# Odd-layer queries and keys: one 512-column matmul for both halves of the tokens, joined by a strided VectorE sum

## The chip, the core and the metric

The kernel runs on one core of a Trainium2 chip. The metric is device time in microseconds, the median of the runs shown. One more execution was taken with the hardware profiler; its own time stands in the table below.

## The reference, cut to what matters

The program is a four-stage encoder trunk over 256 tokens of 1024 features, in float32: an even layer (neighbourhood attention and latent attention), an MLP, an odd layer (three groups of dilated attention), a second MLP. The change touches the projection of the odd layer:

```python
def odd_mixer(xn, w_in, w_o, cos_f, sin_f):
    hcat = (xn @ w_in).reshape(b, s, DIL_GROUPS, 3, DIL_HEADS, HEAD_DIM)
    q = apply_rope(hcat[:, :, :, 0], cos_f, sin_f)
    k = apply_rope(hcat[:, :, :, 1], cos_f, sin_f)
    v = hcat[:, :, :, 2]
    return dilated_attention(q, k, v) @ w_o
```

`apply_rope` rotates pairs of features by the tokens' cosines and sines; `dilated_attention` computes scores, a softmax per group and the weighted values, and mixes the three groups by their softmax denominators.

## The kernel before

Every matrix product is made of three matmuls in a reduced float32 format. Each operand is split into a high half (the rounded value) and a low half (the rest), and `mm3` adds high x high, high x low and low x high into one PSUM bank:

```python
def mm3(o, sh, sl, mh, ml, first, last):
    nc.tensor.matmul(o, sh, mh, start=first, stop=False)
    nc.tensor.matmul(o, sh, ml, start=False, stop=False)
    nc.tensor.matmul(o, sl, mh, start=False, stop=last)
```

The tokens' halves are `xh` and `xl`. Weights come from memory as `raw` tiles in the fixed order of the list `specs`; each is split in four pieces, of which ScalarE writes the high half `whi` (L167) and VectorE the low half `wlo` (L168). Three pairs `whi`, `wlo` exist, so a weight's split waits until TensorE has finished with the weight three places earlier.

The odd layer works in eight units of two heads. Each unit has three query/key weights (b = 0, 1, 2: the queries and keys of the first group, the queries of the other two groups, their keys) and two value weights. A query/key weight gives two results of 128 features x 256 tokens, f = 0 and f = 1, each a chain of eight `mm3` over the eight blocks of features (k); both lie in one PSUM bank, 256 columns each. Then `rope` runs: ScalarE copies four blocks of 32 partitions from the bank into `sw` (L812, L813), VectorE multiplies the bank by the cosines into `r1` (L815) and `sw` by the sines (L816), and adds the two into `q0` (with a split, for b = 0), `q12` or `k12` (L818, L821, L825). The value weights are the moving operand of 384 columns. While TensorE makes the projections of one unit, the attention of the unit before is woven in by `weave`: scores (L180, L848), softmax on VectorE and ScalarE (L855 to L859), transposes of the probabilities (L866) with their copies (L868), and the products with the values (L881, L886) one unit later. On each engine the instructions run in the order that the scheduler gave them when the program was built. Projections and products with the values take turns in four PSUM banks named `acc`.

Of the kernel before, what the change touches and what calls it, by code (L numbers as in the profile page):

```python
# [19 lines left out]
ALU = mybir.AluOpType  # L20
# [24 lines left out]
def trunk(ctx, tc, a, out):  # L45
# [17 lines left out]
    def half_tile(pool, name, bufs, tag="half"):  # L63
        return pool.tile([P, KT, T], F32R, tag=tag, name=name, bufs=bufs)

    def quarter_pair(name):
        return [act.tile([P, KT // 2, T], F32R, tag="quarter", name=name + v, bufs=4) for v in "hl"]
# [107 lines left out]
    def two_heads(o, hi, lo, ts):  # L175

        for n, (y, z) in enumerate(((hi, hi), (hi, lo), (lo, hi))):
            for j in range(2):
                pb = slice(64 * j, 64 * j + 64)
                nc.tensor.matmul(o[j], y[pb, 0, ts], z[pb, 1, :], start=n == 0, stop=n == 2)  # L180
# [23 lines left out]
    def prepare(k, n, xT):  # L204

        hi, lo, gk = xT[0][:, k, :], xT[1][:, k, :], gains[:, n * KT + k:n * KT + k + 1]
        return (lambda: nc.scalar.activation(hi, x[:, k, :], AF.Copy, scale=gk).ins,
                lambda: nc.vector.scalar_tensor_tensor(lo, x[:, k, :], gk, hi.bitcast(F32), ALU.mult, ALU.subtract).ins)
# [62 lines left out]
    def hand_over(accs, last, n, scale=None):  # L271

        xT = half_tile(act, "xh", 2), half_tile(act, "xl", 2)
# [21 lines left out]
    def onto(accs, w, c, v, m, first, last, fbs):  # L295

        for fb in fbs:
            cs = slice(c + fb * P, c + fb * P + P)
            o = accs[fb // 2][:, (fb % 2) * T:(fb % 2) * T + T]
            mm3(o, w[0][:, cs], w[1][:, cs], m[0][v], m[1][v], first and fb % 2 == 0, last and fb % 2 == 1)  # L300

    ALL = slice(None)

    def out_steps(accs, mixed, wo, k):

        def step(fbs):
            if k // 2 not in wo:
                wo[k // 2] = weight()
            onto(accs, wo[k // 2], (k % 2) * D, (ALL, k % 4), mixed[k // 4], k == 0, k == KT - 1, fbs)
        return [lambda fbs=fbs: step(fbs) for fbs in (range(0, 4), range(4, 8))]  # L310

    def out_last(accs, mixed, wo):

        def step(b):
            for k in (6, 7):
                if 3 not in wo:
                    wo[3] = weight()
                onto(accs, wo[3], (k % 2) * D, (ALL, k % 4), mixed[k // 4], False, k == KT - 1, (2 * b, 2 * b + 1))
        return [lambda b=b: step(b) for b in range(4)]

    def mlp(mp, xT, invert, tail, make_down, beside=lambda j: None):
# [4 lines left out]
        def up(j):  # L326
# [4 lines left out]
            for ks in ranges:  # L331
                for f in range(2):
                    for k in ks:
                        c = slice(k * 256 + f * P, k * 256 + f * P + P)
                        mm3(pu[:, f * T:(f + 1) * T], w[0][:, c], w[1][:, c], xT[0][:, k, :], xT[1][:, k, :],
# [5 lines left out]
            hs[j] = tuple(mp.tile([P, 512], F32R, tag=n, name=n, bufs=4) for n in ("hh", "hl"))  # L341
            split(*hs[j], h)
# [15 lines left out]
    def mlp_between(mp, xT, s):  # L358
        def down(accs, hs):
            def step(j, w, f, fbs=range(8)):  # L360
                onto(accs, w, f * D, (ALL, slice(f * T, f * T + T)), hs[j], (j, f) == (0, 0), (j, f) == (15, 1), fbs)
# [11 lines left out]
    def finish(mp, xT, s):  # L373
# [7 lines left out]
        def mm(acc, hs, j, w, f, t, c0, c1, first, last):  # L381
            tk, c = slice(f * T + t * P, f * T + (t + 1) * P), slice(f * D + c0, f * D + c1)
            mm3(acc, hs[j][0][:, tk], hs[j][1][:, tk], w[0][:, c], w[1][:, c], first, last)
# [64 lines left out]
    def even(ep):  # L448
        xT = xh, xl = half_tile(act, "xh", 2), half_tile(act, "xl", 2)
# [28 lines left out]
        cT_h, cT_l = quarter_pair("c")  # L478
# [84 lines left out]
        def qk_steps(c):  # L563
            hold = {}

            def step(f, half):
                if not hold:
                    hold["w"], hold["p"] = weight(), bank("acc" if c else "w")
                (wh, wl), pq = hold["w"], hold["p"]
                for k in range(4 * half, 4 * half + 4):  # L570
                    ws = slice(k * 256 + f * P, k * 256 + f * P + P)
                    mm3(pq[:, f * T:(f + 1) * T], wh[:, ws], wl[:, ws], xh[:, k, :], xl[:, k, :], k == 0, k == KT - 1)
                if f == 1 and half == 1:
                    th, tl = (ep.tile([P, 2, T], F32R, tag=n, name=n, bufs=2) for n in ("qk_h", "qk_l"))
                    q32 = scratch([2, T], "q32")
                    nc.vector.tensor_tensor(q32, pq.rearrange("p (f n) -> p f n", f=2), both, op=ALU.mult)
                    split(th, tl, q32)
                    qk[c] = th, tl
# [7 lines left out]
        def heads_transposed(n, t, h, src):  # L586
# [4 lines left out]
            split(mT[n][0][0:96, hs, tok(t)], mT[n][1][0:96, hs, tok(t)], pt[0:96].rearrange("p (i n) -> p i n", i=4))  # L591

        def uq_steps():
            hold, src = {}, {}

            def gemm(t, h):
                if not hold:
                    hold["w"] = weight()
                    mT["q"] = half_tile(ep, "qh", 2, "mq"), half_tile(ep, "ql", 2, "mq")
# [16 lines left out]
        def ukv_steps():  # L616
            hold, src = {}, {}

            def gemm(t, h):
                if not hold:  # L620
                    hold["w"] = weight()
                    mT["k"] = half_tile(ep, "kh", 2, "mk"), half_tile(ep, "kl", 2, "mk")
# [27 lines left out]
        def scores(n):  # L650
# [5 lines left out]
            if kind == 0:  # L656
                two_heads(sb, *qk[hp], tok(t))
            else:
                for j in range(2):
                    h = 2 * hp + j  # L660
                    (qh, ql), (kh, kl) = mT["q"], mT["k"]
                    mm3(sb[:, j], qh[0:96, h, tok(t)], ql[0:96, h, tok(t)], kh[0:96, h, :], kl[0:96, h, :], True, True)
# [24 lines left out]
        def mix(n):  # L687
# [11 lines left out]
            split(*(z[:, hp, tok(t)] for z in mixed[kind]), pvo[:, 0:P])  # L699
# [47 lines left out]
    def odd(op, xT, s):  # L747
        xh, xl = xT
# [13 lines left out]
        def unit_tiles(u):  # L762
            d = {"k12": k12[u % 2]}
            for n, shape, dt in (("q0h", [P, 2, T], F32R), ("q0l", [P, 2, T], F32R), ("q12", [P, 2, T], F32),
# [29 lines left out]
        def qk_steps(d):  # L794
# [4 lines left out]
            def gemm(b, f, half):  # L799
                if f == 0 and half == 0:  # L800
                    hold["w"], hold["p"] = weight(), bank("acc")
                (wh, wl), pq = hold["w"], hold["p"]
                for k in range(4 * half, 4 * half + 4):
                    ws = slice((f * KT + k) * P, (f * KT + k + 1) * P)
                    mm3(pq[:, f * T:(f + 1) * T], wh[:, ws], wl[:, ws], xh[:, k, :], xl[:, k, :], k == 0, k == KT - 1)
                if f == 1 and half == 1:
                    rope(b, pq)

            def rope(b, pq):
                sw, r1 = scratch([512], "sw"), scratch([2, T], "r1")  # L810
                for r in range(0, P, 64):
                    nc.scalar.copy(sw[r:r + 32], pq[r + 32:r + 64])  # L812
                    nc.scalar.copy(sw[r + 32:r + 64], pq[r:r + 32])  # L813
                sw = sw.rearrange("p (f n) -> p f n", f=2)
                nc.vector.tensor_tensor(r1, pq.rearrange("p (f n) -> p f n", f=2), cosT.unsqueeze(1).broadcast_to([P, 2, T]), op=ALU.mult)  # L815
# [19 lines left out]
        def attention(u, d, other, pause=2):  # L835
# [4 lines left out]
            def scores():  # L840
                ss = {(i, j): bank("w") for i in range(NT) for j in range(2)}
                for i in range(NT):
                    two_heads([ss[i, j][:, 0:T] for j in range(2)], d["q0h"], d["q0l"], tok(i))
# [29 lines left out]
        def mix(u, d, out_tag):  # L873
# [14 lines left out]
            split(*(z[:, u % 4, :] for z in mixed[u // 4]), pvo[:, 0:T])  # L888
# [127 lines left out]
```

## Time and profile before

| what | us |
|---|---|
| median of 3 runs (lowest, highest) | 760.87 (760.02, 761.33) |
| the profiled execution, span from first to last instruction | 759.4 |
| TensorE busy in it | 750.6 |
| VectorE busy | 506.4 |
| ScalarE busy | 499.3 |
| odd layer, from its first to its last matmul of a projection | 302.6 to 542.6 |

The profiler gives the span alone; the median of the runs lies 1.5 us above it. Matmuls overlap in the trace: the time from one start to the next tells what a matmul takes of TensorE, and its own duration is a latency. VectorE's and ScalarE's instructions overlap a little too.

### The profile page before, as it was taken

To read this page: it belongs to the slowest core of one execution; us is meant where nothing else is said; L and a number is where in the kernel's file an instruction comes from. 1 tells how busy PE (TensorE), PEld (TensorE's weight loads), DVE (VectorE), ACT (ScalarE), POOL (GpSimd) and SP (SyncE) were. 2 spreads that over 40 slices of the span, in tenths; PEclk is the share of its full clock that TensorE was granted. 3 is DMA by queue.
4 is the path that set the end of the run, shared out by engine and by line. 5 is a ranking of instruction groups with operands and counts; after the bars stand their busy time and mean duration, and the time that the engine had idled before them with its cause. 6 is when DMAs were issued, how large, how long until landed. Compare 5 with 4: busy or idle time off the path is not lost.

```text
span 759.4 us, 14578 instructions
## 1 busy us (share of the span) xinstructions
PE 750.6 (99%) x5898; PEld 717.1 (94%) x5898; DVE 506.4 (67%) x1033; ACT 499.3 (66%) x1057; POOL 9.5 (1%) x22
## 2 busy tenths in 40 slices
PE   8999999999999999999999999999999999999996
PEld 6898899999999999999999999999999899899895
DVE  6778859646545557887787677786858555555564
ACT  6778977445435435888988889889856554554541
POOL 0100000000000001000000000000000000000000
PEclk9999999999999999999999999999999999999999
DMA  8863334454455544643444444544554555455501
GB/s 280 310 223 139 112 111 162 173 200 177 179 186 179 191 150 170 228 154 136 162 148 153 154 145 169 180 141 163 184 213 148 185 196 176 179 201 174 187 28 55
DMA packets 22818, 129.13 MB, mean 170 GB/s; under 512 B 2912, under 2 KB 5472, under 8 KB 9824
## 3 DMA queue, kind: packets, MB, share of 16 engines
q1 hardware_dynamic: 22464, 127.94, 47.8%
q8 instruction: 46, 0.75, 0.4%
q10 hardware_dynamic: 288, 0.28, 0.1%
q14 instruction: 20, 0.16, 0.1%
HBM read 127.16 MB, written 1.05 MB: 169 GB/s over the span
## 4 chain that ended last, share of the span: by engine, by line
PE 96%; ACT 1%; issue 1%; DMA 1%; DVE 1%; SPq 0%; POOLq 0%; POOL 0%
PE acc L171 21%; PE acc L172 20%; PE acc L173 20%; PE w L171 9%; PE w L172 9%; PE w L173 9%; PE w L180 1%; PE w L866 1%; PE w L683 1%; PE w L848 1%; PE acc L881 1%; PE w L697 1%; DMA raw<-in_w_c 1%; PE w L589 1%; PE acc L697 0%
## 5 line engine op out<-in xcount | busy, mean ns | idle before, releaser
L168 DVE TENSOR_TENSOR wlo<-raw,whi 128x512 fp32r<-128x512 f32 (+3 forms) x488 | 307.0, 663 | 171.9 <-ACT whi L167 171.1
L167 ACT CAST whi<-raw 128x512 fp32r<-128x512 f32 (+3 forms) x488 | 268.6, 599 | 200.0 <-issue 173.8
L172 PE MATMUL w<-xl,whi 128*128 128x256 f32 x528 | 149.2, 283 | 0.0
L173 PE MATMUL w<-xh,wlo 128*128 128x256 f32 x528 | 148.8, 282 | 0.0
L171 PE MATMUL w<-xh,whi 128*128 128x256 f32 x528 | 148.8, 282 | 0.0
L171 PE MATMUL acc<-xh,whi 128*128 128x256 f32 x432 | 125.4, 290 | 0.0
L173 PE MATMUL acc<-xh,wlo 128*128 128x256 f32 x432 | 121.8, 282 | 0.0
L172 PE MATMUL acc<-xl,whi 128*128 128x256 f32 x432 | 121.5, 281 | 0.0
L171 PEld LDWEIGHTS w<-xh,whi 128*128 128x128 f32 x528 | 99.6, 189 | 0.6
L172 PEld LDWEIGHTS w<-xl,whi 128*128 128x128 f32 x528 | 99.2, 188 | 0.6
L173 PEld LDWEIGHTS w<-xh,wlo 128*128 128x128 f32 x528 | 99.7, 189 | 0.0
L171 PEld LDWEIGHTS acc<-xh,whi 128*128 128x128 f32 x432 | 81.1, 188 | 1.3 <-issue 0.3
L172 PEld LDWEIGHTS acc<-xl,whi 128*128 128x128 f32 x432 | 81.8, 189 | 0.0
L173 PEld LDWEIGHTS acc<-xh,wlo 128*128 128x128 f32 x432 | 81.2, 188 | 0.0
L171 PE MATMUL acc<-hh,whi 128*128 128x256 f32 x256 | 72.6, 284 | 0.0
L172 PE MATMUL acc<-hl,whi 128*128 128x256 f32 x256 | 72.4, 283 | 0.0
L173 PE MATMUL acc<-hh,wlo 128*128 128x256 f32 x256 | 72.4, 283 | 0.0
L171 PE MATMUL acc<-whi,xh 128*128 128x384 f32 (+2 forms) x160 | 56.7, 354 | 1.2 <-ACT whi L167 1.2
L172 PE MATMUL acc<-wlo,xh 128*128 128x384 f32 (+2 forms) x160 | 55.9, 349 | 0.2 <-DVE wlo L168 0.2
L173 PE MATMUL acc<-whi,xl 128*128 128x384 f32 (+2 forms) x160 | 55.6, 347 | 0.0
L171 PEld LDWEIGHTS acc<-hh,whi 128*128 128x128 f32 x256 | 49.1, 192 | 0.0
L172 PEld LDWEIGHTS acc<-hl,whi 128*128 128x128 f32 x256 | 49.1, 192 | 0.0
(202 smaller groups left out, 1287.7 us busy)
## 6 DMA issues: line engine op xcount, KB each, us to landing
raw<-in_w SPq DMA_DIRECT2D x64, 1024.0 KB, 4.8
raw<-in_w_oqk SPq DMA_DIRECT2D x24, 1024.0 KB, 4.8
raw<-in_w_ov SPq DMA_DIRECT2D x16, 768.0 KB, 4.3
raw<-in_w_qk SPq DMA_DIRECT2D x4, 1024.0 KB, 10.3
raw<-in_w_oe SPq DMA_DIRECT2D x4, 1024.0 KB, 5.3
raw<-in_w_oo SPq DMA_DIRECT2D x4, 1024.0 KB, 4.8
bias<-in_rpb SPq DMA_DIRECT2D x8, 256.0 KB, 3.7
raw<-in_w_c SPq DMA_DIRECT2D x8, 208.0 KB, 4.9
```

Source lines behind the costliest of these rows:

```text
L167: a = nc.scalar.copy(hi, src).ins
L168: return a, (eng or nc.vector).tensor_tensor(lo, src, hi.bitcast(F32), op=ALU.subtract).ins
L171: nc.tensor.matmul(o, sh, mh, start=first, stop=False)
L172: nc.tensor.matmul(o, sh, ml, start=False, stop=False)
L173: nc.tensor.matmul(o, sl, mh, start=False, stop=last)
L180: nc.tensor.matmul(o[j], y[pb, 0, ts], z[pb, 1, :], start=n == 0, stop=n == 2)
L589: nc.tensor.transpose(pt[0:96, i * P:(i + 1) * P], src[:, i, :], ident)
L683: nc.tensor.transpose(pt[:, b * P:(b + 1) * P], pp[:, b // 2, (b % 2) * P:(b % 2 + 1) * P], ident)
L697: nc.tensor.matmul(pvo[64 * j:64 * j + 64, 0:P], v[:, kk, h * 64:(h + 1) * 64], pts[:, 2 * j + kk, :], start=kk == 0, stop=kk == NT - 1)
L848: nc.tensor.matmul(ss[i, j][rows, T:T + P], d["q12"][:, j, i * P + 64 * c:i * P + 64 * c + 64], d["k12"][:, j, 2 * i + c, :], start=True, ...
L866: nc.tensor.transpose(pt[:, b * P:(b + 1) * P], pp[:, b * P:(b + 1) * P], ident)
L881: nc.tensor.matmul(pvo[cs, tok(i)], d["v0"][:, kk, cs], pts[j][:, kk, :], start=kk == 0, stop=False)
```

## The change

Four things are changed.

1. High and low halves that were two tiles become one tile with a dimension of two, in all stages (`pair_tile`, `halves`). Blocks of 256 columns are then read and written at twice the step. The instructions of the other stages stay the same in kind, size and order.
2. In the odd layer's query/key products, `mm2` takes the place of `mm3`: one matmul of 512 columns takes the high weights against the tokens' high and low halves, which lie side by side, into the whole bank; a second of 256 columns adds low weights x high tokens to the bank's left half.
3. The two halves of the bank must be added: `joined`, one VectorE reduction of 256 pairs that stand 256 elements apart in PSUM, writes the sum to a scratch tile in SBUF.
4. f = 0 and f = 1 have a bank each, so two banks and two reductions per weight; `rope` then reads the scratch tile in SBUF instead of the bank.

```diff
+    def pair_tile(pool, n, name, bufs, tag):
+
+        return pool.tile([P, n, 2, T], F32R, tag=tag, name=name, bufs=bufs)
...
+    def halves(z):
+
+        return (z[:, 0, :], z[:, 1, :]) if len(z.shape) == 3 else (z[:, :, 0, :], z[:, :, 1, :])
...
+    def mm2(o, sh, sl, m, first, last):
+
+        both = lambda: nc.tensor.matmul(o, sh, m.rearrange("p v n -> p (v n)"), start=first, stop=last)
+        low = lambda: nc.tensor.matmul(o[:, 0:T], sl, m[:, 0, :], start=False, stop=False)
+        for step in (low, both) if last else (both, low):
+            step()
+
+    def joined(dst, o):
+
+        nc.vector.tensor_reduce(out=dst, in_=o.rearrange("p (v n) -> p n v", v=2), axis=mybir.AxisListType.X, op=ALU.add)
...
             def gemm(b, f, half):
                 if f == 0 and half == 0:
-                    hold["w"], hold["p"] = weight(), bank("acc")
-                (wh, wl), pq = hold["w"], hold["p"]
+                    hold["w"], hold["s"] = weight(), scratch([2, T], "qk")
+                if half == 0:
+                    hold["p"] = bank("acc")
+                (wh, wl), s, pq = hold["w"], hold["s"], hold["p"]
                 for k in range(4 * half, 4 * half + 4):
                     ws = slice((f * KT + k) * P, (f * KT + k + 1) * P)
-                    mm3(pq[:, f * T:(f + 1) * T], wh[:, ws], wl[:, ws], xh[:, k, :], xl[:, k, :], k == 0, k == KT - 1)
+                    mm2(pq, wh[:, ws], wl[:, ws], xT[:, k], k == 0, k == KT - 1)
+                if half == 1:
+                    joined(s[:, f], pq)
                 if f == 1 and half == 1:
-                    rope(b, pq)
+                    rope(b, s)
...
-            def rope(b, pq):
-                sw, r1 = scratch([512], "sw"), scratch([2, T], "r1")
+            def rope(b, s):
+                sw, r1 = scratch([2, T], "sw"), scratch([2, T], "r1")
                 for r in range(0, P, 64):
-                    nc.scalar.copy(sw[r:r + 32], pq[r + 32:r + 64])
-                    nc.scalar.copy(sw[r + 32:r + 64], pq[r:r + 32])
...
+                    nc.scalar.copy(sw[r:r + 32], s[r + 32:r + 64])
+                    nc.scalar.copy(sw[r + 32:r + 64], s[r:r + 32])
...
-                    split(d["q0h"], d["q0l"], r1)
+                    split(*halves(d["q0"]), r1)
```

On TensorE, in the middle of a query/key weight (`acc` is the bank, `whi` and `wlo` the weight's halves), these matmuls stood before, around the step from one block of features to the next:

```order
L171 MATMUL acc_5911<-xh_3669,whi_5750 128x256
L172 MATMUL acc_5911<-xl_3670,whi_5750 128x256
L173 MATMUL acc_5911<-xh_3669,wlo_5751 128x256
L171 MATMUL acc_5911<-xh_3669,whi_5750 128x256
L172 MATMUL acc_5911<-xl_3670,whi_5750 128x256
```

Now the step from f = 0 to f = 1 on TensorE reads so, with `xT` the tokens' pair tile; the end of f = 0 and the start of f = 1 stand here:

```order
L186 MATMUL acc_5684<-xT_3642,wlo_5535 128x256 x2
L185 MATMUL acc_5684<-xT_3642,whi_5534 128x512
L185 MATMUL acc_5708<-xT_3642,whi_5534 128x512
L186 MATMUL acc_5708<-xT_3642,wlo_5535 128x256
L185 MATMUL acc_5708<-xT_3642,whi_5534 128x512
```

Three matmuls have become two, the bank changes between f = 0 and f = 1, and in the last block of a chain the 512 columns come last, so two matmuls of 256 columns meet there.

On VectorE, in a middle unit, from the end of the softmax (`drz` are its reciprocals) on through the rope of b = 0, these rows stood before. The `wlo` of 128x384 are the splits of the next value weight, `pts` the copy of transposed probabilities:

```order
L858 RECIPROCAL drz_5838<-dz_5837 128x1
L858 RECIPROCAL drz_5847<-dz_5846 128x1
L168 TENSOR_TENSOR wlo_5984<-raw_5748,whi_5983 128x384
L868 COPY pts_5928<-w_5924 128x384
L815 TENSOR_TENSOR r1_5889<-acc_5760,cosT_3810 128x512
L816 TENSOR_TENSOR sw_5888<-sw_5888,sinT_3811 128x512
L168 TENSOR_TENSOR wlo_5984<-raw_5748,whi_5983 128x384
L818 TENSOR_TENSOR r1_5889<-r1_5889,sw_5888 128x512
L168 TENSOR_TENSOR wlo_5984<-raw_5748,whi_5983 128x384 x2
L168 TENSOR_TENSOR q0l_5744<-r1_5889,q0h_5743 128x512
```

Now the same place of VectorE's queue, with the line numbers of the changed kernel (L176 for L168, L835 for L815, L836 for L816, L838 for L818, L192 the reduction):

```order
L878 RECIPROCAL drz_5619<-dz_5618 128x1
L192 TENSOR_REDUCE qk_5544<-acc_5545 128x256
L878 RECIPROCAL drz_5628<-dz_5627 128x1
L192 TENSOR_REDUCE qk_5544<-acc_5642 128x256
L176 TENSOR_TENSOR wlo_5744<-raw_5532,whi_5743 128x384
L835 TENSOR_TENSOR r1_5661<-qk_5544,cosT_3782 128x512
L176 TENSOR_TENSOR wlo_5744<-raw_5532,whi_5743 128x384
L888 COPY pts_5697<-w_5693 128x384
L836 TENSOR_TENSOR sw_5660<-sw_5660,sinT_3783 128x512
L192 TENSOR_REDUCE qk_5683<-acc_5684 128x256
L838 TENSOR_TENSOR r1_5661<-r1_5661,sw_5660 128x512
L176 TENSOR_TENSOR wlo_5744<-raw_5532,whi_5743 128x384 x2
```

Both reductions of b = 0 stand between the softmax and the first split; the cosine product and the second split have moved ahead of the place where ScalarE's copies are waited for; and a reduction of b = 1 follows the sine product.

## Rows read from the trace of the kernel before

**Rows 1.** The page: span, busy time of each engine, TensorE's clock in tenths.

```profile
span 759.4 us, 14578 instructions
PE 750.6 (99%) x5898; PEld 717.1 (94%) x5898; DVE 506.4 (67%) x1033; ACT 499.3 (66%) x1057; POOL 9.5 (1%) x22
PEclk9999999999999999999999999999999999999999
```

**Rows 2.** Windows, one unit: length; PE, PEld, DVE, ACT, POOL busy (count); clock; DMA.

```profile
451.19:481.58 30.39, 30.39 (x267) 30.02 (x266) 22.52 (x49) 26.59 (x57) 0.00 (x0) 1.00 0.46 156
```

**Rows 3.** Timeline of TensorE, b = 2: start, duration; matmuls 1 and 31.

```profile
465.83 0.28 PE L173 MATMUL acc<-xh,wlo 128*128 128x256 f32 x1
...
469.43 0.28 PE L173 MATMUL acc<-xh,wlo 128*128 128x256 f32 x1
```

**Rows 4.** The same view at 512 columns: 1 and 24 (second MLP); 1 and 26 (even layer).

```profile
702.89 0.39 PE L171 MATMUL acc<-whi,hh 128*128 128x512 f32 x1
...
708.15 0.39 PE L173 MATMUL acc<-whi,hl 128*128 128x512 f32 x1
...
23.01 0.39 PE L171 MATMUL acc<-whi,xh 128*128 128x512 f32 x1
...
28.87 0.39 PE L172 MATMUL acc<-wlo,xh 128*128 128x512 f32 x1
```

**Rows 5.** Groups by form, whole span: busy us, mean ns, idle before.

```profile
L168 DVE TENSOR_TENSOR wlo<-raw,whi 128x512 fp32r<-128x512 f32 x408 | 265.7, 685 | 159.8 <-ACT whi L167 159.1 <-issue 0.3
L167 ACT CAST whi<-raw 128x512 fp32r<-128x512 f32 x408 | 231.8, 618 | 190.1 <-issue 167.3 <-PE acc L173 11.3 <-PE acc L172 5.7
L812 ACT COPY sw<-acc 32x512 f32<-32x512 f32 x48 | 27.8, 579 | 0.9
L815 DVE TENSOR_TENSOR r<-acc,cosT 128x512 f32<-128x512 f32 x24 | 16.6, 692 | 28.7 <-ACT sw L813 28.7
L671 DVE TENSOR_SCALAR_CACHE_REDUCE sn<-w 128x256 f32<-128x256 f32 x16 | 6.2, 418 | 1.3 <-PE w L173 1.3
```

**Rows 6.** Waits, 360.02 to 511.97: us in total, times, longest.

```profile
DVE wlo L168 <- ACT whi L167: 18.4, 16, 1.4
DVE r L815 <- ACT sw L813: 16.6, 15, 1.3
```

**Rows 7.** Timeline of VectorE in the unit 451 to 482; idle before in brackets.

```profile
459.92 0.16 DVE L858 RECIPROCAL drz<-dz 128x1 f32<-128x1 f32 x1 [0.58 <-ACT pp L857]
461.33 0.56 DVE L168 TENSOR_TENSOR wlo<-raw,whi 128x384 fp32r<-128x384 f32 x1 [1.25 <-ACT whi L167]
463.70 0.69 DVE L815 TENSOR_TENSOR r<-acc,cosT 128x512 f32<-128x512 f32 x1 [1.34 <-ACT sw L813]
464.31 0.68 DVE L816 TENSOR_TENSOR sw<-sw,sinT 128x512 f32<-128x512 f32 x1
469.53 0.69 DVE L815 TENSOR_TENSOR r<-acc,cosT 128x512 f32<-128x512 f32 x1 [1.00 <-ACT sw L813]
471.81 1.62 DVE L168 TENSOR_TENSOR wlo<-raw,whi 128x384 fp32r<-128x384 f32 x3
474.42 0.69 DVE L815 TENSOR_TENSOR r<-acc,cosT 128x512 f32<-128x512 f32 x1 [0.99 <-ACT sw L813]
476.23 1.38 DVE L825 TENSOR_TENSOR k<-r,sw 64x512 f32<-64x512 f32 x2
```

**Rows 8.** Timeline of ScalarE at the same place.

```profile
460.80 0.50 ACT L167 CAST whi<-raw 128x384 fp32r<-128x384 f32 x1
463.69 1.34 ACT L167 CAST whi<-raw 128x384 fp32r<-128x384 f32 x3
```

**Rows 9.** Timeline of TensorE: first matmul with the unit's second value weight.

```profile
473.40 0.34 PE L171 MATMUL acc<-whi,xh 128*128 128x384 f32 x1
```

**Rows 10.** Timelines of the first unit: keys written (VectorE), first read (TensorE).

```profile
334.34 1.38 DVE L825 TENSOR_TENSOR k<-r,sw 64x512 f32<-64x512 f32 x2
336.13 0.44 PE L848 MATMUL w<-k,q 128*64 128x128 f32 x4
```

More of the change, by code (lines that the diff above doesn't have):

```diff
@@ L293, in open_accs, with onto @@
         return [bank("acc") for _ in range(4)]
-    def onto(accs, w, c, v, m, first, last, fbs):
+    def onto(accs, w, c, m, first, last, fbs):
         for fb in fbs:
@@ L299, in onto @@
             o = accs[fb // 2][:, (fb % 2) * T:(fb % 2) * T + T]
-            mm3(o, w[0][:, cs], w[1][:, cs], m[0][v], m[1][v], first and fb % 2 == 0, last and fb % 2 == 1)
-    ALL = slice(None)
+            mm3(o, w[0][:, cs], w[1][:, cs], *halves(m), first and fb % 2 == 0, last and fb % 2 == 1)
     def out_steps(accs, mixed, wo, k):
@@ L340, in up @@
             nc.vector.tensor_tensor(h, r, pu, op=ALU.mult)
-            hs[j] = tuple(mp.tile([P, 512], F32R, tag=n, name=n, bufs=4) for n in ("hh", "hl"))
-            split(*hs[j], h)
+            hs[j] = pair_tile(mp, 2, "h", 4, "h")
+            split(*halves(hs[j]), two(h))
         for j in range(3):
@@ L360, in step @@
             def step(j, w, f, fbs=range(8)):
-                onto(accs, w, f * D, (ALL, slice(f * T, f * T + T)), hs[j], (j, f) == (0, 0), (j, f) == (15, 1), fbs)
+                onto(accs, w, f * D, hs[j][:, f], (j, f) == (0, 0), (j, f) == (15, 1), fbs)
             return step
@@ L381, in mm @@
         def mm(acc, hs, j, w, f, t, c0, c1, first, last):
-            tk, c = slice(f * T + t * P, f * T + (t + 1) * P), slice(f * D + c0, f * D + c1)
-            mm3(acc, hs[j][0][:, tk], hs[j][1][:, tk], w[0][:, c], w[1][:, c], first, last)
+            c = slice(f * D + c0, f * D + c1)
+            mm3(acc, hs[j][:, f, 0, tok(t)], hs[j][:, f, 1, tok(t)], w[0][:, c], w[1][:, c], first, last)
         def down(accs, hs):
@@ L568, in step @@
                     hold["w"], hold["p"] = weight(), bank("acc" if c else "w")
[L569 removed]
+                (wh, wl), pq = hold["w"], two(hold["p"])
                 for k in range(4 * half, 4 * half + 4):
                     ws = slice(k * 256 + f * P, k * 256 + f * P + P)
[L572 removed]
+                    mm3(pq[:, f], wh[:, ws], wl[:, ws], *halves(xT[:, k]), k == 0, k == KT - 1)
                 if f == 1 and half == 1:
[L574 removed]
+                    qk[c] = pair_tile(ep, 2, "qk", 2, "qk")
                     q32 = scratch([2, T], "q32")
[L576 to L578 removed]
+                    nc.vector.tensor_tensor(q32, pq, both, op=ALU.mult)
+                    split(*halves(qk[c]), q32)
             return [lambda f=f, h=h: step(f, h) for f in range(2) for h in range(2)]
@@ L590, in heads_transposed @@
             hs = slice(4 * h, 4 * h + 4)
-            split(mT[n][0][0:96, hs, tok(t)], mT[n][1][0:96, hs, tok(t)], pt[0:96].rearrange("p (i n) -> p i n", i=4))
+            split(*(mT[n][0:96, hs, v, tok(t)] for v in range(2)), pt[0:96].rearrange("p (i n) -> p i n", i=4))
         def uq_steps():
@@ L698, in mix @@
                                      start=kk == 0, stop=kk == NT - 1)
-            split(*(z[:, hp, tok(t)] for z in mixed[kind]), pvo[:, 0:P])
+            split(*(mixed[kind][:, hp, v, tok(t)] for v in range(2)), pvo[:, 0:P])
         def attention():
@@ L842, in scores @@
                 for i in range(NT):
-                    two_heads([ss[i, j][:, 0:T] for j in range(2)], d["q0h"], d["q0l"], tok(i))
+                    two_heads([ss[i, j][:, 0:T] for j in range(2)], d["q0"], tok(i))
                 for i in range(NT):
@@ L887, in mix @@
                                          start=False, stop=c == 1)
-            split(*(z[:, u % 4, :] for z in mixed[u // 4]), pvo[:, 0:T])
+            split(*halves(mixed[u // 4][:, u % 4]), pvo[:, 0:T])
         d, nd = unit_tiles(0), unit_tiles(1)
```

46 lines of the change are left out of this document (22 added, 24 removed).

## Prediction

> **What bounds the kernel now.** I read the page first: TensorE is busy for 750.6 of 759.4 us, its weight loads for 717.1, VectorE and ScalarE for two thirds each, and TensorE's clock stands at 9 tenths or more in every slice [rows 1]. The median of the runs, 760.87, lies 1.5 us over that span, so differences are worked out on the span and taken off the median. "Busy" says little of an engine whose matmuls overlap, so the next view is the windows of one unit of the odd layer: 30.39 us, of which TensorE is busy for all 30.39 at clock 1.00, VectorE for 22.52 and ScalarE for 26.59 [rows 2]. TensorE sets the pace there and waits for nobody; what it saves per matmul comes off the end, as long as the other two keep up. So two questions decide: what the new pair of matmuls takes from start to start, and whether VectorE has room for six more instructions per unit.
>
> **What leaves TensorE.** The starts of 31 matmuls of 256 columns in a row span 3.60 us, so one takes 3.60 / 30 = 0.1200 us [rows 3]. The odd layer has 8 units x 3 weights x 2 results x 8 blocks = 384 triples, each 3 x 0.1200 = 0.3600. The new pair is one matmul of 256 columns, 0.1200, and one of 512. For 512 the trace has two stretches: in the second MLP 24 of them start over 5.26 us, 0.2286 each; in the even layer 26 over 5.86 us, 0.2344 each [rows 4]. I take 0.2286: its stretch alternates with 256-column runs under a VectorE and ScalarE load like the odd layer's, while the other stands beside the heavy loading at the start. The pair is then 0.3486, the triple loses 11.4 ns, and 384 of them 4.4 us. With 0.2344 it is 5.6 ns and 2.2 us. The upper bound comes from the rows of 256 and 512 themselves: if 256 columns more cost only their share at one column per cycle of 2.4 GHz, 0.1067, then 512 takes 0.2267, the triple loses 13.3 ns, and the sum is 5.1 us. So the saving is what one matmul costs beyond its columns; the columns themselves are the same 768.
>
> The Trainium skill, "TensorE: Matmul & The Clock Gate", section "Back-to-back issue gap", puts that fixed part at about 2.5 ns per warm matmul. By it 384 matmuls fewer would bring 384 x 2.5 ns = 1.0 us, as an estimate. The trace does not agree: 0.1200 is 13.3 ns over 256 columns at 2.4 GHz [rows 3].
>
> **What comes onto VectorE.** 48 reductions, six per unit, each reading 512 elements of PSUM. No row has this instruction. From below: an instruction that reads 256 elements of PSUM and accumulates takes 418 ns; a product that reads 512 from PSUM takes 692 [rows 5]. From above: if the step of 256 elements made each read cost twice, two such products, 1.38 us. I take the 692 of the 512 elements, because the reduction has to read as many; in a queue such instructions follow each other at 0.61 us (463.70 to 464.31 [rows 7]), so 6 x 0.60 = 3.6 us per unit, 22.5 + 3.6 = 26.1 of a unit that is to last 30.39 - 48 x 0.0114 = 29.8.
>
> The Trainium skill, "VectorE: DVE Perf Modes", section "Rules for kernel authors", speaks against the change: it calls `tensor_reduce` the slowest VectorE operation on a hot path and advises restructuring. Its rate of one element per cycle is also that of the 692 ns product, so by the page the price above stands; whether the strided read adds to it no row shows.
>
> **Where the 3.6 us fit.** VectorE's idle time in a unit is 7.9 us, and most of it is waiting for ScalarE: over five units 18.4 us for `whi` and 16.6 for the rope's copies `sw` [rows 6]. The new order fills just these holes. Walked with these durations through the unit from 451 us: VectorE ends the softmax at 459.3 (459.92 less 0.58 idle [rows 7]), makes both reductions of b = 0 by 460.65 (TensorE has left them: b = 1's 48 matmuls and two sets of transposes, some 6.3 us, lie between them and b = 2, which begins six matmuls before 465.83, at 465.1 [rows 3]), and meets the first split piece at 461.33 as before [rows 7], since ScalarE's cast starts at 460.80 [rows 8]. ScalarE makes a second cast and the four copies until 464.2; VectorE meanwhile does the cosine product, a split and the copy `pts` (463.3), waits 1.0 instead of 1.34 us, and goes on with sine product, a reduction of b = 1 (465.5), sum (466.1), two splits, `q0`'s low half, the other reduction (468.25), two splits, cosine product, split, the first reduction of b = 2, and the last split of the second value weight at 471.3. Before, that split ended at about 472.8 (second of the three from 471.81 [rows 7]); its first use is at 473.40 [rows 9], and that weight's last quarter is needed nine matmuls later still. The keys `k12` end at 478.0 against 477.6 (476.23 + 1.38), and the scores that read them come after the unit's end at 481.58. TensorE arrives 0.28 us earlier at each query/key weight's end and 0.55 at the unit's. So the reductions cost nothing on the path while the holes hold them; without that cover they would cost 3.6 us in each unit.
>
> **Waits that the change adds.** ScalarE's copies now wait for a reduction instead of TensorE, with the value weight's casts and the next copies queued behind them; in the walk the reductions end at 460.65, 468.3 and 473.1, the copies are reached at 461.7, 468.5 and 473.1. So no loss, but no slack in the third. They also read SBUF instead of PSUM: a cast from SBUF of as many columns takes 618 ns against the copy's 579 [rows 5], 12 x 0.04 = 0.5 us per unit, which ScalarE has (26.6 + 0.5 of 29.8). TensorE waits for banks: a unit now takes nine turns of the four, not six. The tightest is the second half of b = 1, which needs the bank of b = 0's first half back: that reduction ends at 459.9, TensorE comes there at about 461.6 (24 matmuls and a set of transposes, 3.2 us, before 465.1, less the 0.3 saved). Nothing, with 1.7 us to spare.
>
> One place is tight, the first unit: `k12` ends at 334.34 + 1.38 = 335.72 and TensorE reads it at 336.13 [rows 10]. TensorE will be there 64 triples x 11.4 ns = 0.7 us earlier, at 335.4, and VectorE has the reductions in between; I put 0 to 0.6 us on it and take 0.2, once. The pair tiles change no order or size in the other stages, and blocks of 256 columns stay unbroken: nothing.
>
> **Sum.** 4.4 - 0.2 = 4.2 us: the span falls from 759.4 to 755.2, the median from 760.87 to 756.7.
>
> **Rivals.**
> 1. *512 columns cost what they cost in the even layer.* Rows 4 have it, beside a heavy load of the memory; the odd layer's load is half of the queues' time [rows 2], which speaks against. Saving 2.2 - 0.2: 758.9.
> 2. *No change.* The fixed part of a matmul may belong not to the instruction but to something that grows with the columns: at 512 columns the even layer has 21 ns of it, at 256 columns 13 [rows 3, 4]. At 27 ns, twice 13.3, nothing is saved. Or waits of about 0.5 us per unit on the third copies eat it. Then 760 to 761, say 760.5; 0.05 for the first way, 0.07 for the second. The estimate from the page above, 1.0 us, would come out here too, at 759.9.
> 3. *VectorE becomes the bound: slower.* If the strided read doubles the reduction to 1.2 us in the queue, VectorE needs 22.5 + 7.2 = 29.7 per unit, and some 1.6 us of its waits for `sw` stay (1.0 and 0.6 in the walk): 31.3 against 30.39, seven full units, +6.4: about 767. It decides from (30.39 - 22.5 - 1.6) / 6 = 1.05 us per reduction on; below 0.95 TensorE still leads. For it speaks only that no row shows a read of PSUM with a step.
>
> **How the numbers follow.** My forecast 0.66; rival 1 0.10; rival 2 0.12; rival 3 0.12. A measurement tells 0.2%, 1.5 us, from no change. The forecast and rival 1 are faster by more (0.76), rival 2 is the same (0.12), rival 3 slower (0.12). The range starts at the full 13.3 ns, 760.87 - 5.1 = 755.8, less the runs' spread of some 0.4, 755.4; above it takes in rivals 1 and 2, to 760.6, and leaves out rival 3 and the worst part of the second, some 0.15.
>
> **What the profile will show.** Right: pairs of starts 0.12 and 0.23 apart in the odd layer, 384 matmuls fewer, units of 29.8 us with TensorE busy throughout; reductions of about 0.69 us, VectorE at 26 us per unit, no TensorE wait on L192 or `wlo`. Wrong: reductions above 0.95 us, TensorE waiting for an `acc` bank or a value weight, units at 30.4 or longer; or 512 columns at 0.234 and more.

## The result, and the profile after

The changed kernel takes 761.45 us (760.83 to 762.12, 20 runs) beside 760.27 of the kernel before: a ratio of 1.0014 [1.0007, 1.002]. The forecast was 756.7, and the range ended at 760.6. So the saving did not come, and the time lies a little above that of before. The page of the profiled execution, to be read beside [rows 1]:

```profile
span 759.7 us, 13864 instructions
PE 748.7 (99%) x5514; PEld 694.7 (91%) x5514; DVE 531.7 (70%) x1075; ACT 503.3 (66%) x1063; POOL 9.4 (1%) x22
PE 90%; ACT 3%; DVE 3%; issue 2%; DMA 1%; SPq 0%; POOLq 0%; POOL 0%
```

TensorE has 384 matmuls fewer, as the change says. VectorE has 42 instructions more and ScalarE 6, because the 48 reductions came and the scheduler gave six of the 32 copies `pts` of 384 columns to ScalarE that VectorE had. The third line, the chain that ended last, shows the news: ScalarE and VectorE hold 3% of it each. Before, the same line had 1% for each:

```profile
PE 96%; ACT 1%; issue 1%; DMA 1%; DVE 1%; SPq 0%; POOLq 0%; POOL 0%
```

The groups by form (answering to [rows 5]) show that the added work has its forecast price, 679 ns for the reduction and 618 ns for a copy from SBUF:

```profile
L192 DVE TENSOR_REDUCE qk<-acc 128x256 f32<-128x512 f32 x48 | 32.6, 679 | 0.0
L833 ACT COPY sw<-qk 32x512 f32<-32x512 f32 x48 | 29.7, 618 | 3.0 <-DVE qk L192 2.3
```

Now the pace. The timeline of TensorE, at the first scores with `k12` of six units in a row, where each unit should begin 29.8 us after the last:

```profile
389.71 0.33 PE L868 MATMUL w<-k,q 128*64 128x128 f32 x2
...
419.76 0.33 PE L868 MATMUL w<-k,q 128*64 128x128 f32 x2
...
449.81 0.33 PE L868 MATMUL w<-k,q 128*64 128x128 f32 x2
...
480.10 0.33 PE L868 MATMUL w<-k,q 128*64 128x128 f32 x2
...
510.80 0.33 PE L868 MATMUL w<-k,q 128*64 128x128 f32 x2
...
544.06 0.33 PE L868 MATMUL w<-k,q 128*64 128x128 f32 x2
```

The same instruction in the kernel before, first, third and the last two:

```profile
391.25 0.33 PE L848 MATMUL w<-k,q 128*64 128x128 f32 x2
...
452.03 0.33 PE L848 MATMUL w<-k,q 128*64 128x128 f32 x2
...
512.81 0.33 PE L848 MATMUL w<-k,q 128*64 128x128 f32 x2
544.88 0.33 PE L848 MATMUL w<-k,q 128*64 128x128 f32 x2
```

At first TensorE is faster, 30.05 us per unit (389.71 to 419.76, then to 449.81) against 30.39, and 2.22 us ahead by the third row (452.03 - 449.81). Then its units take 30.29, 30.70 and, with the start of the output projection in between, 33.26 against 32.07, and the lead is down to 0.82 us; the span ends 0.3 us behind (759.7 against 759.4).

Not all of this lead comes from the change. The first matmul of the odd layer, in the kernel before and then in the changed one, already starts 0.78 us apart:

```profile
302.64 0.34 PE L171 MATMUL acc<-whi,xh 128*128 128x384 f32 x1
301.86 0.34 PE L179 MATMUL acc<-whi,xT 128*128 128x384 f32 x1
```

The profiled execution of the kernel before had lost time at its start. Its window from 8 to 12 us shows a granted clock of 0.57, so most of that stretch ran at the lower level (1.2 GHz), after TensorE had been busy for 0.77 of the 2.00 us before; the changed kernel has 1.00 there.

```profile
8.00:12.00 4.00, 3.83 (x12) 3.51 (x12) 3.66 (x9) 4.00 (x11) 0.00 (x0) 0.57 0.94 246
```

Counted from the first matmul of the odd layer, the changed kernel is 1.44 us ahead at 449.81, 0.04 at 544.06, and 1.1 behind at the end, which is what the medians say (761.45 - 760.27 = 1.18). VectorE's timeline, at the first scaled copy `v0` of successive units, has the 30.70 in every unit:

```profile
386.90 0.34 DVE L803 TENSOR_SCALAR v<-acc,rstd 128x128 f32<-128x128 f32 x1
...
417.60 0.34 DVE L803 TENSOR_SCALAR v<-acc,rstd 128x128 f32<-128x128 f32 x1
...
448.30 0.34 DVE L803 TENSOR_SCALAR v<-acc,rstd 128x128 f32<-128x128 f32 x1
...
479.00 0.34 DVE L803 TENSOR_SCALAR v<-acc,rstd 128x128 f32<-128x128 f32 x1
```

Two paces, 30.05 and 30.70: TensorE runs ahead of the other two by 0.65 us a unit until what they prepare for it is not ready. From 302 to 570 us its waits add up to 3.0 us, where the kernel before shows none. Where it then stands, the timeline of TensorE shows with the idle time in brackets: at the transposes of a late unit, and twice in the last attention, where a bank is not yet read out by ScalarE:

```profile
488.78 0.55 PE L886 MATMUL w<-ident,pp 128*128 128x128 f32 x3 [0.42 <-ACT pp L879]
...
542.24 0.39 PE L179 MATMUL acc<-oa,whi 128*128 128x256 f32 x1 [0.69 <-ACT v L807]
...
546.75 0.39 PE L179 MATMUL acc<-oa,whi 128*128 128x256 f32 x1 [0.69 <-ACT v L807]
```

And the waits from 360.02 to 511.97 (us in total, times, longest), which answer to [rows 6]:

```profile
DVE wlo L176 <- ACT whi L175: 15.2, 14, 1.4
DVE sw L836 <- ACT sw L834: 8.1, 10, 0.9
ACT v L806 <- DVE v L803: 7.7, 5, 1.6
ACT q L175 <- DVE r L838: 5.0, 5, 1.0
```

ScalarE and VectorE wait for each other alone. In the kernel before they waited for TensorE too (ScalarE 7.6 us in all, VectorE 1.9), as the same view of it shows:

```profile
ACT whi L167 <- PE acc L173: 7.6, 5, 1.5
ACT v L789 <- DVE v L786: 2.6, 5, 0.5
DVE v L786 <- PE acc L173: 1.9, 5, 0.4
```

Those waits are gone, and ScalarE's wait for `v0` has grown from 2.6 to 7.7. That is the theory tested below: the two engines, with their queues in a fixed order and each waiting for the other, go round once per unit in 30.70 us, and this loop took the pace over from TensorE. Neither is full: in a window of one unit's length (its length first, then TensorE, its weight loads, VectorE and ScalarE) VectorE is busy for 25.57 us and ScalarE for 27.15.

```profile
390.02:420.71 30.69, 30.69 (x234) 28.05 (x230) 25.57 (x54) 27.15 (x58) 0.00 (x0) 1.00 0.44 154
```

### The profile page after: what moved, and what is told of

Same layout as the page of the kernel before. It is cut to its first block, busy times and chain, and to the rows that moved or that the text cites. A ratio compares the mean times of both kernels' runs of the same rounds, so it can differ in the third digit from the quotient of the medians.

```text
span 759.7 us, 13864 instructions
## 1 busy us (share of the span) xinstructions
PE 748.7 (99%) x5514; PEld 694.7 (91%) x5514; DVE 531.7 (70%) x1075; ACT 503.3 (66%) x1063; POOL 9.4 (1%) x22
## 3 DMA queue, kind: packets, MB, share of 16 engines
HBM read 127.16 MB, written 1.05 MB: 169 GB/s over the span
## 4 chain that ended last, share of the span: by engine, by line
PE 90%; ACT 3%; DVE 3%; issue 2%; DMA 1%; SPq 0%; POOLq 0%; POOL 0%
PE acc L179 14%; PE acc L180 13%; PE acc L181 13%; PE acc L185 10%; PE w L179 9%; PE w L180 9%; PE w L181 9%; PE acc L186 5%; PE w L886 1%; DMA raw<-in_w_c 1%; DVE wlo L176 1%; PE w L199 1%; ACT whi L175 1%; PE w L700 1%; PE w L714 1%
## 5 line engine op out<-in xcount | busy, mean ns | idle before, releaser
L176 DVE TENSOR_TENSOR wlo<-raw,whi 128x512 fp32r<-128x512 f32 (+3 forms) x488 | 308.3, 662 | 171.4 <-ACT whi L175 170.7
L180 PE MATMUL w<-xT,whi 128*128 128x256 f32 x528 | 149.2, 283 | 0.0
L181 PE MATMUL w<-xT,wlo 128*128 128x256 f32 x528 | 148.9, 282 | 0.0
L179 PE MATMUL w<-xT,whi 128*128 128x256 f32 x528 | 148.9, 282 | 0.0
L185 PE MATMUL acc<-xT,whi 128*128 128x512 f32 x384 | 137.2, 401 | 0.0
L179 PEld LDWEIGHTS w<-xT,whi 128*128 128x128 f32 x528 | 99.5, 189 | 0.6
L180 PEld LDWEIGHTS w<-xT,whi 128*128 128x128 f32 x528 | 99.2, 188 | 0.6
L186 PE MATMUL acc<-xT,wlo 128*128 128x256 f32 x384 | 99.7, 280 | 0.0
L181 PEld LDWEIGHTS w<-xT,wlo 128*128 128x128 f32 x528 | 99.6, 189 | 0.0
L179 PE MATMUL acc<-h,whi 128*128 128x256 f32 x256 | 72.6, 284 | 0.0
L180 PE MATMUL acc<-h,whi 128*128 128x256 f32 x256 | 72.5, 283 | 0.0
L181 PE MATMUL acc<-h,wlo 128*128 128x256 f32 x256 | 72.5, 283 | 0.0
L179 PE MATMUL acc<-whi,xT 128*128 128x384 f32 (+2 forms) x160 | 56.6, 354 | 0.4 <-ACT whi L175 0.4
L181 PE MATMUL acc<-whi,xT 128*128 128x384 f32 (+2 forms) x160 | 55.3, 346 | 0.0
L179 PEld LDWEIGHTS acc<-h,whi 128*128 128x128 f32 x256 | 49.1, 192 | 0.0
L180 PEld LDWEIGHTS acc<-h,whi 128*128 128x128 f32 x256 | 49.1, 192 | 0.0
```

Source lines behind the costliest of these rows:

```text
L176: return a, (eng or nc.vector).tensor_tensor(lo, src, hi.bitcast(F32), op=ALU.subtract).ins
L185: both = lambda: nc.tensor.matmul(o, sh, m.rearrange("p v n -> p (v n)"), start=first, stop=last)
L186: low = lambda: nc.tensor.matmul(o[:, 0:T], sl, m[:, 0, :], start=False, stop=False)
```

## The experiments

Each run was measured beside the kernel before. "Loop" is the time between successive first `v0` (or first softmax steps) in the middle units, "TensorE" that between its scores there while it waits for nobody.

| run | edit | us | ratio to before | loop | TensorE |
|---|---|---|---|---|---|
| (change) | | 761.45 | 1.0014 [1.0007, 1.002] | 30.70 | 30.05 |
| e1_pairs_only | no merged matmul, no sum | 760.1 | 0.9998 [0.999, 1.0007] | 30.39 | 30.39 |
| e2_three_matmuls_and_sum | sum without merged matmul | 765.65 | 1.0072 [1.006, 1.0084] | 31.25 | 30.39 |
| e3_left_half | shorter sum | 765.06 | 1.0064 [1.0051, 1.0077] | 31.24 | waits in each unit |
| e4_v0_scalar | `v0` on ScalarE | 757.65 | 0.9968 [0.9956, 0.998] | 30.35 | 30.05 |
| e5_v0_scalar_before | the same, kernel before | 759.87 | 0.9996 [0.9987, 1.0006] | 30.39 | 30.39 |
| e6_sum_twice | each sum twice | 766.4 | 1.0083 [1.0069, 1.0097] | uneven | uneven |
| e7_v0_scalar_grouped | e4, 512 columns in a row | 757.79 | 0.9969 [0.9957, 0.998] | 30.35 | 30.07 |
| e8_sum_priority | sums earlier in the queue | 763.08 | 1.0042 [1.0029, 1.0054] | 31.10 | 30.05 |
| e9_v0_priority | `v0` earlier in the queue | 758.03 | 0.9973 [0.9963, 0.9983] | 30.17 | 30.05 |
| e10_copies_pool | half the copies on GpSimd | 773.13 | 1.0168 [1.0155, 1.0182] | 31.85 | waits in each unit |
| e11_v0_priority_before | e9's edit, kernel before | 759.73 | 0.9994 [0.9985, 1.0003] | 30.39 | 30.39 |

**One part at a time.** First the tiles alone, then the sums alone.

```diff
-                    hold["w"], hold["s"] = weight(), scratch([2, T], "qk")
-                if half == 0:
-                    hold["p"] = bank("acc")
+                    hold["w"], hold["p"] = weight(), two(bank("acc"))
...
-                    mm2(pq, wh[:, ws], wl[:, ws], xT[:, k], k == 0, k == KT - 1)
+                    mm3(pq[:, f], wh[:, ws], wl[:, ws], *halves(xT[:, k]), k == 0, k == KT - 1)
...
-                if half == 1:
-                    joined(s[:, f], pq)
...
-                    rope(b, s)
+                    rope(b, pq)
```

> The changed kernel with its pair tiles, but the odd layer's queries and keys again by three matmuls of 256 columns into one bank, and the rotation read from that bank as before. Loop theory (ScalarE and VectorE wait for each other in a loop of 30.7 us per unit that the sums made longer than TensorE's work): no sums, so the loop is short again, units of 30.39 us led by TensorE, 760.3, as the kernel before. Pair theory (the loop does not decide; the merged matmuls or the new tiles do): also 760.3 if the matmuls are to blame, 761 or more if the tiles are.

```diff
+    def mm4(o, sh, sl, m, first, last):
+        nc.tensor.matmul(o[:, 0:T], sh, m[:, 0, :], start=first, stop=False)
+        nc.tensor.matmul(o[:, 0:T], sl, m[:, 0, :], start=False, stop=False)
+        nc.tensor.matmul(o[:, T:2 * T], sh, m[:, 1, :], start=False, stop=last)
```

> The changed kernel with its sums and its bank per result, but three matmuls of 256 columns: hi x hi and lo x hi into the left half of the bank, hi x lo into the right half. TensorE's work per unit is that of before, 30.39 us. Loop theory: the loop with the sums in it is 30.7 us and leads in each of some seven units, 7 x 0.3 = 2.1 us more than before, and the last attention some 0.3: 762.7, units of 30.7 in every unit, ScalarE never waiting for TensorE. Pair theory: the sums lie in idle time, units 30.39, 760.3 to 760.8.

The tiles cost nothing (760.1), as the prediction had it. The sums alone, with TensorE's work as before, cost more than the loop theory said: 765.65, because the loop is 31.25 and not 30.7. The scheduler had ordered ScalarE's and VectorE's queues anew for this kernel (VectorE has 16 of the 32 copies `pts` of 384 columns, and 9 in the changed kernel), so the loop is not one fixed number that the sums bring along.

**A shorter sum.**

```diff
-        nc.vector.tensor_reduce(out=dst, in_=o.rearrange("p (v n) -> p n v", v=2), axis=mybir.AxisListType.X, op=ALU.add)
+        nc.vector.tensor_copy(out=dst, in_=o[:, 0:T])
```

> The changed kernel whose sum is a copy of the bank's left half alone, so the product of high weights and low tokens is left out of queries and keys; TensorE's instructions are those of the changed kernel. A copy that reads 256 columns should take some 0.42 us, not 0.68: 6 x 0.26 = 1.6 us of VectorE's work per unit less. Loop theory: half of that or more comes off the loop, 30.7 - 0.8 = 29.9 or less, so TensorE's 30.05 leads again: units of 30.05, 757.5 to 759. Pair theory: 761.4, as the changed kernel.

Both theories missed: 765.06. The copy takes 416 ns (median), as expected, and VectorE has less to do, but the loop grew to 31.24. The window of one unit of this kernel:

```profile
388.70:419.93 31.23, 30.42 (x218) 27.28 (x217) 24.54 (x55) 26.64 (x57) 0.00 (x0) 1.00 0.43 152
```

VectorE's 24.54 and ScalarE's 26.64 are both below those of the changed kernel, in a unit that is 0.54 us longer. The loop is there, now in every unit (TensorE itself stands idle for 0.8 us of it), but its length is not given by the amount of work. Its queues differ from the changed kernel's at several places, a copy `pts` more per unit on VectorE among them. So the theory took a second form: the order of the two queues sets the loop, by where one engine stands still for the other.

**The wait for `v0`.** The largest stop of ScalarE, 1.6 us per unit, is removed by making `v0` on ScalarE; then the same in the kernel before.

```diff
-                nc.vector.tensor_scalar(d["v0"][:, i, :], pq[:, 0:P], ri, None, ALU.mult)
+                nc.scalar.activation(d["v0"][:, i, :], pq[:, 0:P], AF.Copy, scale=ri)
```

> The changed kernel with the scaled copy of the first value group (v0) on ScalarE instead of VectorE, nothing left out. ScalarE's wait for VectorE there, 1.6 us per unit, goes, for two copies of some 0.36 us on ScalarE. Loop theory: the loop loses some 0.9 us, 30.7 to 29.8, TensorE's 30.05 leads: 757.5 to 759. Pair theory: 761.4, as the changed kernel.

> The kernel before with the scaled copy v0 on ScalarE, the same edit as in the run on the changed kernel that took 757.65. Loop theory: here TensorE leads (ScalarE waits 1.5 us per unit for it), so the edit gives nothing in the units, at most some 0.3 us in the last attention: 760.0 to 760.3, and the 2.6 us between this kernel and that one are what the merged matmuls save once nothing takes it back. Rival: the edit is worth its 2.6 to 3.8 us in any kernel and the merged matmuls save nothing: 757.7.

757.65 and 759.87: in the changed kernel the edit brings 3.8 us, in the kernel before nothing that the runs resolve. TensorE keeps its 30.05 through all middle units, since a loop of 30.35 falls behind too slowly to catch it before they end. So the merged matmuls do save, and the loop had eaten it. Between these two runs lie 2.2 us.

**More work, another order.**

```diff
+        nc.vector.tensor_reduce(out=dst, in_=o.rearrange("p (v n) -> p n v", v=2), axis=mybir.AxisListType.X, op=ALU.add)
```

> The changed kernel with each sum made twice into the same place: 6 x 0.60 = 3.6 us more of VectorE's work per unit, TensorE and ScalarE unchanged. VectorE's work is then 25.3 + 3.6 = 28.9 of TensorE's 30.05. Capacity theory (an engine holds the others up only when its own work fills the unit): no change, 761.5. Loop theory: the sums lie in a loop with no slack, so the unit grows by half to all of the 3.6 us, to 32.5 to 34.3, in eight units: 776 to 790.

766.4 is a miss for both: 5 us more than with single sums, not 15 to 29. Six sums more fit into a unit at a fraction of their price, since they took up time in which VectorE had waited: its waits for `whi` and `sw` from 390 to 520 us fall from 22.8 us in the changed kernel to 6.4, and it is nearly full (29.02 of 30 us from 390 to 420). That the sums lie in a loop "with no slack" was wrong.

```diff
-                    joined(s[:, f], pq)
+                    with tc.high_priority(20):
+                        joined(s[:, f], pq)
```

> The changed kernel with the sums given a little priority, so that they stand earlier in VectorE's queue (ahead of the sine product, the second copy of transposed weights falls to VectorE); the same instructions and work, nothing but their order. It asks why the run with the shorter sums was slower than the changed kernel. If the order of the two queues sets the loop: a unit longer or shorter than 30.69 by 0.2 us or more, here rather near the 31.24 of that run, whose queue it resembles: 764 to 765. If the amount of work sets it: 761.4.

763.08, between the two numbers, with a loop of 31.10. The order moved the loop by 0.4 us, but the scheduler also gave four of the 32 copies `pts` of 384 columns to VectorE that ScalarE had, so this is not order alone. The next one is: the counts of instructions on both engines are those of the changed kernel (1075 and 1063), and the copies `pts` are shared as there.

```diff
-                nc.vector.tensor_scalar(d["v0"][:, i, :], pq[:, 0:P], ri, None, ALU.mult)
+                with tc.high_priority(60):
+                    nc.vector.tensor_scalar(d["v0"][:, i, :], pq[:, 0:P], ri, None, ALU.mult)
```

> The changed kernel with priority for the scaled copy v0, so that VectorE makes it ahead of the keys k12 in its queue and not behind them; the same instructions and work on every engine. Loop theory in its second form (what decides is where one engine stands still for the other in the order of the two queues, above all ScalarE's 1.6 us per unit for v0): that wait shrinks by about the 1.4 us of k12, the loop falls from 30.69 to near TensorE's 30.05: 757.6 to 758.6. Work theory (the v0 edit helped because VectorE had less to do): 761.4.

> The kernel before with the same priority for v0. Loop theory: TensorE leads here, so a shorter wait for v0 gives nothing in the units and at most some 0.3 us in the last attention: 759.9 to 760.3; what is left to the 758.03 of the changed kernel with that priority, 1.9 to 2.3 us, is the saving of the merged matmuls. Rival: the order alone is worth the 2.2 us, whatever the matmuls: 758.0.

758.03 and 759.73. VectorE's timeline at that place in the changed kernel, with `k12` ahead of `v0`:

```profile
446.28 1.38 DVE L845 TENSOR_TENSOR k<-r,sw 64x512 f32<-64x512 f32 x2
447.69 0.69 DVE L176 TENSOR_TENSOR wlo<-raw,whi 128x512 fp32r<-128x512 f32 x1
448.30 0.34 DVE L803 TENSOR_SCALAR v<-acc,rstd 128x128 f32<-128x128 f32 x1
```

and ScalarE's there, whose copies `v12` of the same bank stand behind `v0`:

```profile
446.43 0.62 ACT L175 CAST whi<-raw 128x512 fp32r<-128x512 f32 x1
448.68 0.36 ACT L806 ACTIVATE v<-acc,rstd 64x128 f32<-64x128 f32 x1 [1.62 <-DVE v L803]
```

With priority, VectorE:

```profile
443.65 0.69 DVE L176 TENSOR_TENSOR wlo<-raw,whi 128x512 fp32r<-128x512 f32 x1
444.26 0.34 DVE L804 TENSOR_SCALAR v<-acc,rstd 128x128 f32<-128x128 f32 x1
444.52 1.38 DVE L846 TENSOR_TENSOR k<-r,sw 64x512 f32<-64x512 f32 x2
```

and ScalarE, which goes from the copy `pts` into `v12` with no stop that the view marks:

```profile
444.04 0.47 ACT L889 COPY pts<-w 128x384 f32<-128x384 f32 x1
444.64 0.36 ACT L807 ACTIVATE v<-acc,rstd 64x128 f32<-64x128 f32 x1
```

Its window of one unit, in which VectorE and ScalarE have as much work as in the changed kernel (25.80 and 27.25 us), is 30.17 us long and not 30.69:

```profile
391.83:422.00 30.17, 30.17 (x219) 27.52 (x218) 25.80 (x55) 27.25 (x57) 0.00 (x0) 1.00 0.45 157
```

TensorE's timeline then holds its pace, 30.05 a unit to the end of the middle units:

```profile
449.55 0.44 PE L869 MATMUL w<-k,q 128*64 128x128 f32 x4
...
479.60 0.44 PE L869 MATMUL w<-k,q 128*64 128x128 f32 x4
...
509.64 0.44 PE L869 MATMUL w<-k,q 128*64 128x128 f32 x4
```

Order alone is worth 3.4 us in the changed kernel (761.45 to 758.03), and nothing that the runs resolve in the kernel before. It is not `v0`'s place alone: other instructions moved with it (VectorE's third softmax step follows the second after 0.55 us, and after 1.14 in the changed kernel), and how the 3.4 us divide among them was not separated. Like e4, this version beats both kernels, with nothing left out.

**Another relief.**

```diff
-                    nc.scalar.copy(sw[r + 32:r + 64], s[r:r + 32])
+                    nc.gpsimd.tensor_copy(out=sw[r + 32:r + 64], in_=s[r:r + 32])
```

> The changed kernel with two of the four swapped copies of each rotation on GpSimd, which is idle there; v0 stays on VectorE. They run beside ScalarE's two, so the rotation's copies take 1.3 us, not 2.5, if GpSimd takes no longer for one of 32x512 than ScalarE. Loop theory: VectorE's waits for the copies (1.9 us per unit) go or shrink, the loop falls below 30.4: 757.6 to 759. If GpSimd takes twice as long or more, the copies set the loop as before or worse: 761.4 or above.

773.13. One copy takes GpSimd 973 ns, 1.6 times ScalarE's 618; two in a row are still shorter than ScalarE's four, and yet the loop is 31.85. ScalarE has less work and waits more (3.3 us per unit for `v0`, 3.0 for the sums). How much of that is the new order, how much the slower copies, and how much VectorE's instructions that took longer in this run (last section) was not separated.

**The price of 512 columns.** On top of e4, four of 512 columns and four of 256 in a row:

```diff
-                for k in range(4 * half, 4 * half + 4):
-                    ws = slice((f * KT + k) * P, (f * KT + k + 1) * P)
-                    mm2(pq, wh[:, ws], wl[:, ws], xT[:, k], k == 0, k == KT - 1)
+                def wide():
+                    for k, c in zip(ks, ws):
+                        nc.tensor.matmul(pq, wh[:, c], xT[:, k].rearrange("p v n -> p (v n)"), start=k == 0, stop=k == KT - 1)
...
+                def low():
+                    for k, c in zip(ks, ws):
+                        nc.tensor.matmul(pq[:, 0:T], wl[:, c], xT[:, k, 0, :], start=False, stop=False)
...
+                for step in (low, wide) if half else (wide, low):
+                    step()
```

> The kernel with v0 on ScalarE (757.65, where TensorE leads everywhere), with the matmuls of a half regrouped: four of 512 columns in a row and four of 256 in a row, not in turn; the same sums and the same result. It asks why 512 columns took 0.233 us here and not the forecast 0.2286. If that comes of alternating with 256 columns (in one bank, on the same left half): 0.2286, 384 x 4.4 ns = 1.7 us less, 756.0. If it belongs to 512 columns with these operands: 757.6.

757.79: nothing changed. The timeline of TensorE shows eight of 512 columns between 455.30 and 457.17, 1.87 / 8 = 0.234 each, so they cost the same in a row as alternating:

```profile
455.30 2.03 PE L827 MATMUL acc<-xT,whi 128*128 128x512 f32 x8
457.17 0.64 PE L831 MATMUL acc<-xT,wlo 128*128 128x256 f32 x4
```

## Why the prediction was wrong

**The step that failed is "So the reductions cost nothing on the path while the holes hold them".** The holes did hold them. But the walk asked the wrong question at its end. It found that `k12` ends at 478.0 us against 477.6, and let that pass because the scores come after 481.58. In a unit that repeats, the question is not whether TensorE still finds its input in this unit, but how long the two engines take to come round. Here the forecast's own numbers gave the warning: the keys end 0.4 us later in a unit that was to be 0.55 shorter, so the two engines lose almost 1 us per unit on TensorE. Taken as they stand they give a loop of 30.39 + 0.4 = 30.8, and 30.70 was measured; that the two are so near is luck, as the two parts below show. TensorE ran ahead until the row at 449.81 before the loss showed in its pace; whether a shorter layer would have hidden it, no run shows.

The walk was also too short by 0.5 us. From the first softmax step to the end of `k12` the kernel before took 22.73 us, from 454.88 in its timeline of VectorE to 476.23 + 1.38 [rows 7]:

```profile
454.88 0.55 DVE L855 CUSTOM_DVE_ANT_0 sn<-w,mask 128x384 f32<-128x384 f32 x1
...
485.27 0.55 DVE L855 CUSTOM_DVE_ANT_0 sn<-w,mask 128x384 f32<-128x384 f32 x1
```

The changed kernel took 23.64, to 476.99 + 1.38, so 0.91 us more and not 0.4:

```profile
454.73 0.55 DVE L875 CUSTOM_DVE_ANT_0 sn<-w,mask 128x384 f32<-128x384 f32 x1
...
476.99 1.38 DVE L845 TENSOR_TENSOR k<-r,sw 64x512 f32<-64x512 f32 x2
...
485.43 0.55 DVE L875 CUSTOM_DVE_ANT_0 sn<-w,mask 128x384 f32<-128x384 f32 x1
```

From there to the next softmax it is 7.06 us after against 7.66 before. In the kernel before, the waits for TensorE stood in this part (ScalarE's from the end of `pts` to 478.10, VectorE's before 480.18), and they fell away. The two parts add up to 30.70 and 30.39. The walk stopped at `k12` and never looked at `v0`, behind which ScalarE's `v12`, the casts and the next softmax are queued; "Waits that the change adds" has no word of it, and it was the one to which e9 gave priority.

**The size of the saving.** A second step failed in size. "I take 0.2286" chose the wrong one of the two rows: in the odd layer 512 columns take 0.233 to 0.234, near rival 1's price. A pair starts every 0.352 us in TensorE's timeline, (427.15 - 425.04) / 6:

```profile
425.04 0.39 PE L185 MATMUL acc<-xT,whi 128*128 128x512 f32 x1
...
427.15 0.39 PE L185 MATMUL acc<-xT,whi 128*128 128x512 f32 x1
```

So a triple loses 8 ns and not 11.4 (the 256 columns of a pair take 0.118, a little less than 0.1200). Over a unit TensorE gains 30.39 - 30.05 = 0.34 us, 2.7 us over eight, where the forecast had 4.4. One sum of the walk does not come out of the forecast's own numbers either: 16 triples at 11.4 ns bring TensorE 0.18 us per query/key weight and not 0.28, which changed nothing else. With the loop out of the way the runs give 1.7 (e9 against e11), 2.2 (e4 against e5) and 2.5 us (e4 against e1). Rival 1's saving, 2.0 us, is near what the change is worth by itself; its reason, the heavy load of the memory, is not borne out by the trace of the changed kernel. Of 338 starts behind a matmul of 512 columns in the odd layer, sorted by the DMA share of the 2 us around them, the third with the least load (share 0.04 on average) and the third with the most (0.80) both follow after 0.233 us.

**What held.** 384 matmuls fewer; the reduction at 679 ns (forecast 0.69); the copies 0.04 us longer; no wait for a bank on account of the sums; the pair tiles free (e1). The first unit's `k12` made TensorE wait 0.5 us, inside the 0 to 0.6 given, above the 0.2 taken.

**The rivals.** Rival 3 had the right end, that TensorE loses the lead, but not the way: it set the point at 1.05 us per sum, from VectorE's work plus 1.6 us of waits, and with 0.68 us the lead was lost. Its sum let the engine's work fill the unit. e6, with twice the sums and VectorE almost full, was only 5 us slower, and e9, with the work unchanged, 3.4 faster: neither follows from work alone. Rival 2 came nearest in time, through waits, but put them on the third copies; those waited 0.3 us a unit.

Open stays which stops make up the 31.24 of e3 and the 31.85 of e10; the order of a queue could not be held fixed while its work was changed.

## What to carry to other kernels

When a repeating stage is led by one engine and that engine gets faster, work out how long the other engines take to come round once, with their waits for each other but without their waits for the leader, and compare that with the leader's new pace; a busy share of 83% (VectorE) or 88% (ScalarE), as here, is no sign of room. A finding of the kind "ends 0.4 us later, but still in time" is a loss per repetition once the repetition gets shorter. And where a scheduler orders the queues, an edit changes the order too: an instruction behind which another engine stands can be worth more than the work that was saved, and is moved for nothing.

## What the runs showed of the hardware

A reduction that adds pairs 256 elements apart in PSUM took 679 ns for 512 elements read; the cosine product of 512 elements took 683 from SBUF in the same kernel and 692 from PSUM in the kernel before [rows 5]. So the stride added nothing that these rows show. The Trainium skill, "VectorE: DVE Perf Modes", section "Rules for kernel authors", calls `tensor_reduce` the slowest operation of VectorE; these numbers do not agree.

A matmul of 512 columns took 0.233 us in the odd layer in turn with one of 256 and 0.234 in a row, against 0.2286 in the second MLP [rows 4], at the same granted clock of 1.00. The load of the DMA engines made no difference in the odd layer; why the two prices differ is open.

In e10, where GpSimd makes half of the copies, VectorE's cosine product took 875 ns on average instead of 683, as its groups show. The average hides two times: 13 of the 24 took 0.68 to 0.69 us and 11 took 1.10 or 1.11. Each of the 11 overlaps a copy on GpSimd in the timeline, but so do eight of the 13; what decides between them is open.

```profile
L834 POOL COPY sw<-qk 32x512 f32<-32x512 f32 x48 | 46.7, 973 | 187.8 <-DVE qk L192 186.8
L835 DVE TENSOR_TENSOR r<-qk,cosT 128x512 f32<-128x512 f32 x24 | 21.0, 875 | 0.0
```
